# Hybrid decoder layer: the split parts of the attention heads stacked along the rows of the matmul

## The chip, the cores and the metric

The kernel runs on one core of a Trainium2 chip. The metric is the time of one execution on the device, in microseconds (us). Five engines work side by side and meet through semaphores: PE (TensorE, matmuls, with PEld its weight loads), DVE (VectorE), ACT (ScalarE), POOL (GpSimd), and SP, which issues the DMAs. Each engine takes its instructions in order.

## The reference, cut to what matters

One decoder layer, 512 tokens of width 1,024, float32. A combined projection of the normed input, `h @ w_in`, feeds three causal token mixers, an RWKV-7 branch, forgetting attention (the code says fox) and latent attention (mla). Their outputs are gated and merged; an MLP follows. The change lies in the two attentions.

```
# forgetting attention: 4 heads of 64
log_f = jax.nn.log_sigmoid((f + b_forget).astype(jnp.float32))
cum = jnp.cumsum(log_f, axis=1)
s = einsum(q, k) * 64 ** -0.5
s = s + cum[t] - cum[s]            # the decay, per head
# latent attention: 4 heads, 128 columns without position and 64 with rope
s = einsum(concat(q_nope, q_pe), concat(k_nope, k_pe)) * 192 ** -0.5
# both, per block of 128 queries
s = jnp.where(k_pos <= q_pos, s, MASK_VALUE)
p = jax.nn.softmax(s, axis=-1);  o = p @ v
```

## The kernel before

**Split numbers.** A product in float32 is made from float32r parts: `hilo` writes the high part of a tile (ACT) and the rest (DVE), and `mm3` multiplies high by high, high by low and low by high (lines 148 to 150), three passes into one PSUM bank. One *block* is one `mm3` of 128 rows by 512 columns.

**Start.** `startup` norms the input and makes seven 128-row slices of the projection in PSUM (`zps`): five latent slices, and query and key of the first pair of forgetting heads. `attn_inputs` then makes the token-major part (`pn`: values of the forgetting heads, forget logits, rope key), the norms of the latents, query and key of the second pair (`zz`, eight blocks each), and the cumulative log forget (`forget_cumsum`), whose high and low parts for all four heads lie in the rows of `cq` and `ck`.

**Attention loop.** `attention` runs 34 steps: eight heads (0 to 3 forgetting, 4 to 7 latent) times four query blocks j. Step k computes the logits of block k (L_k, keys 0 to 128(j+1)) and its softmax on DVE and ACT, runs filler work, then the product with the values of the head that ended two steps ago (`attend`, every fourth step), then the transposes of the block before (T_(k-1)). The order of PE's instructions is the order in the code; the other engines are ordered by the framework's scheduler from data dependencies.

**Forgetting logits.** The two heads of a pair share a tile, one in rows 0 to 63 and one in rows 64 to 127, so the three passes of a head run on 64 rows. A fourth pass of 128 rows adds the decay (`cq` by `ckh`, where `ckh` picks the head's rows of `ck`), a fifth (identity by mask) the causal mask. The value product takes 128 columns of values, both heads of a pair, in three passes and keeps the 64 rows of its own head.

**Latent logits.** Three passes of 128 rows, then q1 by k1 (high query over both halves, key high and low stacked: 128 rows), then q2 by k1 on 64 rows (low query by high key), then the mask.

**Filler work.** `self.fillers` is a list of (first step, generator). `fill(us)` adds credit and takes pieces from the head of the list while credit lasts and the head's first step has come; credit that finds nothing is dropped. A block is worth `MM3` = 0.64. The amounts are `FILL_0` = 3.9 (before L0, and again in step 0), then per step `FILL_A` = 1.85 plus `FILL_J[k % 4]` = 0.2, -0.2, 0.05, -0.3, and 0.2 more from step 16. `finish(g)` runs the list until g is used up. The pieces are `z_steps(i)`, a 128-row slice of the projection for RWKV (eight blocks); `mla_prep` (rope, queries); `key_norms`; `mla_up(i)`, query and key of latent head i (transposes and five blocks); `mla_values`; and gate slices. Weights come from `self.feed` in the same order, one piece ahead (`weight`): a DMA of 512 KB, then the split into `whi` and `wlo` on ACT and DVE.

```
def finish(self, steps):
    while any(s is steps for _, s in self.fillers):
        next(self.fillers[0][1], None) or self.drop()
```

The buffers that matter: `qk` (queries and keys) has 12, `wk` (softmax rows and scratch) 5, the logits (`sc`) 2, `tp` and `pv` one each, `acc` 3.

## Time and profile before

| | |
|---|---|
| median of 3 runs | 887.59 us (887.14 to 890.51) |
| the profiled execution | 887.63 us, its span 885.9 us |
| PE, PEld | 869.3 us (98%), 706.5 us (80%) |
| DVE, ACT, POOL | 518.8 us (59%), 375.2 us (42%), 98.5 us (11%) |
| granted TensorE clock | 0.993 |
| chain that ended last | PE 89%, DVE 6%, ACT 1%, DMA 1%, issue 1% |
| attention loop | about 99.5 to 242 us of the span |

The span runs from the first to the last instruction. Busy time adds up the intervals of an engine's instructions; matmuls are pipelined, so PE's rows overlap each other. A timeline row gives the start, the duration, the engine, the line, the operation, the tile written, the tiles read, the shape (rows\*columns of the weights and rows x columns of the moving data), and in brackets the idle time before it and what ended it.

### The profile page before, as it was taken

The page shows a single profiled execution, that of the slowest core. Times are in us where ns is not written, and L with a number is a line of the kernel's source. Part 1 is how long each engine was busy: PE and PEld are TensorE (multiplying, and loading weights), DVE is VectorE, ACT ScalarE, POOL GpSimd, SP SyncE. Part 2 cuts the span into 40 slices and gives each one's busy share as a digit, 9 for nine tenths or more (in the row PEclk, how much of TensorE's full clock was granted, in tenths as well). Part 3 has the DMA queues.
Part 4 walks back from the last instruction along what each step waited for, and adds up shares of the span by engine and source line. Part 5 has one row for each costly group of instructions (what it writes and reads, how often), then busy time and mean ns, then how long its engine had stood idle before and what let it go on. Part 6 is the DMA issues. An engine that isn't in the chain of part 4 may idle for free.

```text
span 885.9 us, 12143 instructions
## 1 busy us (share of the span) xinstructions
PE 869.3 (98%) x4568; PEld 706.5 (80%) x4568; DVE 518.8 (59%) x1038; ACT 375.2 (42%) x843; POOL 98.5 (11%) x131
## 2 busy tenths in 40 slices
PE   8889999999999999999999999999999999999997
PEld 6679787877877888886788899888888888888886
DVE  6998775676489765344586696442236543233455
ACT  5357554655462232324654775331314332112331
POOL 4510040000021199100000110000000000000000
PEclk9999999999999999999999999999999999999999
DMA  9764220111246833311147312333346432333311
GB/s 358 231 229 150 74 63 32 53 50 46 91 142 181 280 110 90 113 49 48 32 116 260 118 63 65 116 94 85 104 145 199 132 119 83 96 107 96 95 48 72
DMA packets 32636, 102.57 MB, mean 116 GB/s; under 512 B 5873, under 2 KB 7553, under 8 KB 31810
## 3 DMA queue, kind: packets, MB, share of 16 engines
q1 hardware_dynamic: 32002, 100.94, 36.0%
q0 software_dynamic: 288, 0.79, 0.4%
q8 instruction: 36, 0.59, 0.3%
q14 instruction: 22, 0.18, 0.1%
q10 hardware_dynamic: 288, 0.08, 0.0%
HBM read 99.15 MB, written 2.63 MB: 115 GB/s over the span
## 4 chain that ended last, share of the span: by engine, by line
PE 89%; DVE 6%; ACT 1%; DMA 1%; issue 1%; SPq 0%; DVEq 0%; ACTq 0%
PE acc L148 24%; PE acc L150 24%; PE acc L149 24%; DVE wm L220 1%; PE z L473 1%; PE tp L684 1%; DVE wlo L464 1%; PE sc L148 1%; DVE mod L429 1%; DMA xt<-xT 1%; DVE hl L465 1%; PE sc L717 1%; PE sc L806 1%; PE sc L149 1%; DMA wm<-wmod 1%
## 5 line engine op out<-in xcount | busy, mean ns | idle before, releaser
L121 DVE TENSOR_TENSOR wlo<-wraw,whi 128x512 fp32r<-128x512 f32 (+4 forms) x260 | 167.0, 661 | 209.2 <-ACT whi L120 208.8
L120 ACT ACTIVATE whi<-wraw 128x512 fp32r<-128x512 f32 (+4 forms) x260 | 145.2, 586 | 306.2 <-PE acc L149 180.3
L148 PE MATMUL acc<-g,whi 128*128 128x512 f32 (+1 forms) x304 | 109.4, 360 | 0.0
L150 PE MATMUL acc<-g,wlo 128*128 128x512 f32 (+1 forms) x304 | 109.2, 359 | 0.0
L149 PE MATMUL acc<-g,whi 128*128 128x512 f32 (+1 forms) x304 | 109.2, 359 | 0.0
L148 PE MATMUL acc<-hh,whi 128*128 128x512 f32 x256 | 104.6, 408 | 0.0
L149 PE MATMUL acc<-wlo,uh 128*128 128x512 f32 (+1 forms) x262 | 102.1, 390 | 0.0
L150 PE MATMUL acc<-whi,ul 128*128 128x512 f32 (+1 forms) x262 | 102.0, 389 | 0.0
L148 PE MATMUL acc<-whi,uh 128*128 128x512 f32 (+1 forms) x262 | 102.0, 389 | 0.0
L150 PE MATMUL acc<-hh,wlo 128*128 128x512 f32 x256 | 100.3, 392 | 0.3 <-DVE wlo L121 0.3
L149 PE MATMUL acc<-hl,whi 128*128 128x512 f32 x256 | 100.0, 391 | 0.0
L148 PEld LDWEIGHTS acc<-g,whi 128*128 128x128 f32 x304 | 57.3, 188 | 9.4
L150 PEld LDWEIGHTS acc<-g,wlo 128*128 128x128 f32 x304 | 57.3, 188 | 9.3
L149 PEld LDWEIGHTS acc<-g,whi 128*128 128x128 f32 x304 | 57.3, 188 | 9.2
L220 DVE SCALAR_TENSOR_TENSOR wm<-wm,crow 128x1024 f32<-128x1024 f32 x41 | 50.2, 1225 | 23.2 <-DMA wm<-wmod 23.2
L149 PEld LDWEIGHTS acc<-wlo,uh 128*128 128x128 f32 x262 | 49.3, 188 | 11.6 <-DVE wlo L121 0.4
L148 PEld LDWEIGHTS acc<-whi,uh 128*128 128x128 f32 x262 | 49.3, 188 | 11.1
L150 PEld LDWEIGHTS acc<-whi,ul 128*128 128x128 f32 x262 | 49.3, 188 | 11.1
L150 PEld LDWEIGHTS acc<-hh,wlo 128*128 128x128 f32 x256 | 48.1, 188 | 11.4 <-DVE wlo L121 0.8
L148 PEld LDWEIGHTS acc<-hh,whi 128*128 128x128 f32 x256 | 48.5, 189 | 10.3 <-issue 0.2
L149 PEld LDWEIGHTS acc<-hl,whi 128*128 128x128 f32 x256 | 48.3, 189 | 8.4
L673 ACT ACTIVATE p<-sc,nb 128x128 f32<-128x128 f32 (+3 forms) x32 | 16.8, 525 | 30.0 <-DVE nb L669 16.5
(443 smaller groups left out, 1497.7 us busy)
## 6 DMA issues: line engine op xcount, KB each, us to landing
wm<-wmod SPq DMA_DIRECT2D x36, 512.0 KB, 4.6
wraw<-wu SPq DMA_DIRECT2D x32, 512.0 KB, 3.7
wraw<-wd SPq DMA_DIRECT2D x24, 512.0 KB, 3.5
wraw<-wgb SPq DMA_DIRECT2D x16, 512.0 KB, 3.7
wm<-wmod SPq DMA_DIRECT2D x6, 1024.0 KB, 6.6
wraw<-wz SPq DMA_DIRECT2D x10, 512.0 KB, 3.6
wraw<-wga SPq DMA_DIRECT2D x8, 512.0 KB, 3.6
wraw<-wo SPq DMA_DIRECT2D x8, 512.0 KB, 4.4
```

The costliest lines, as they stand in the source:

```text
L120: nc.scalar.activation(hi, src, AF.Copy)
L121: nc.vector.tensor_tensor(lo, src, hi.bitcast(F32), ALU.subtract)
L148: mm(out, lhs[0], rhs[0], start=start, stop=False)
L149: mm(out, lhs[0], rhs[1], start=False, stop=False)
L150: mm(out, lhs[1], rhs[0], start=False, stop=stop)
L220: self.nc.vector.scalar_tensor_tensor(w, w, 0.5, self.crow[:, cols], ALU.mult, ALU.mult, accum_out=dst)
L429: nc.vector.scalar_tensor_tensor(A, acc[0], b1[:, d:d + 1], self.col("gpre", d), ALU.add, ALU.mult)
L464: nc.vector.tensor_tensor(wlo, raw, whi.bitcast(F32), ALU.subtract)
L465: nc.vector.scalar_tensor_tensor(lo, t, B, hi.bitcast(F32), ALU.add, ALU.subtract)
L473: nc.tensor.matmul(zps[i], w[:, i * P:(i + 1) * P], r, start=first and w is whi and r is hi, stop=last and r is lo)
L673: nc.scalar.activation(p[:, 0:n], ps[:, 0:n], AF.Exp, bias=nb, scale=scale, accum_out=den)
L684: nc.tensor.transpose(tp[:, kb, :], p[:, kb * P:(kb + 1) * P], self.ident)
```

## The change

Queries and keys of each forgetting head get four tiles of 128 rows of their own (`fqa`, `fqb`, `fka`, `fkb`). In `fqa` the head's own 64 rows hold the high part of the query and the other 64 the low part; `fka` holds the high part of the key in both halves. In `fqb` and `fkb` the own rows hold the query's high and the key's low part, and the other rows the decay (`fox_decay`, from `cum` by two constant columns). Two passes of 128 rows then give what four gave. The values of a head are stored as 64 high and 64 low columns side by side; two passes, by the high and by the low part of the probabilities, give a high half and a low half of the output, which `attend` adds. The latent `q2` is stored in both halves, so its pass has 128 rows. Query and key of the second pair move from `attn_inputs` into the filler list (`fox_steps`, from step 4, finished before head 2), and z slices 0 and 1 take their place. `key_norms` is put between the blocks of z[4]. In the constants, `sel` is replaced by `cmul` and `cadd`. The fill amounts stay.

```diff
     def attn_inputs(self, pz, zps):
...
+        self.omu = self.cp.tile([P, 8], F32, name="omu")
+        nc.vector.tensor_scalar(self.omu, self.col("mu", 0, 8), -1.0, 1.0, ALU.mult, ALU.add)
...
-        self.fv = [[self.vt(f"fv{q}{i}") for i in range(2)] for q in "hl"]
+        self.fv = [self.vt(f"fv{t}") for t in range(NT)]
...
-        self.fq = [None, None]
-        self.fk = [None, None]
-        self.fq[0] = (self.qk("fq0h"), self.qk("fq0l"))
-        self.fk[0] = (self.qk("fk0h"), self.qk("fk0l"))
-        self.hilo(*self.fq[0], zps[5], 0.125)
-        self.hilo(*self.fk[0], zps[6])
+        self.fqk = [None] * 4
+        self.fox_queries(0, zps[5])
+        self.fox_keys(0, zps[6])
...
-            vl = slice((t % 2) * 256, (t % 2) * 256 + 256)
-            self.hilo(self.fv[0][t // 2][:, vl], self.fv[1][t // 2][:, vl], pn[t][:, 0:256])
+            fv = self.fv[t].rearrange("p (h q f) -> p h q f", h=4, q=2)
+            self.hilo(fv[:, :, 0], fv[:, :, 1], pn[t][:, 0:256].rearrange("p (h f) -> p h f", h=4))
...
-        gen = self.stream(a["wz"][:, 0:2 * D], D)
-        for i, (dst, name, sc) in enumerate(((self.fq, "fq1", 0.125), (self.fk, "fk1", None))):
+        self.ksq = []
+        self.feed = self.pieces([(a["wz"][:, (2 + i) * D:(3 + i) * D], D) for i in range(2)] + self.attn_weights())
+        self.ahead = None
+        self.weight()
+        for i in range(2):
...
-            for kb, _ in enumerate(self.block_steps(ps, next(gen), h, range(NB))):
+            for kb, _ in enumerate(self.z_steps(i, ps)):
...
-            if i == 0:
-                self.feed = self.pieces(self.attn_weights())
-                self.ahead = None
-            dst[1] = (self.qk(name + "h"), self.qk(name + "l"))
-            self.hilo(*dst[1], ps, sc)
-        self.weight()
...
+    def fox_queries(self, pair, ps):
+        nc = self.nc
+        for hh in range(2):
+            own, oth = slice(hh * 64, hh * 64 + 64), slice(64 - hh * 64, 128 - hh * 64)
+            qa, qb, ka, kb = self.fqk[2 * pair + hh] = [self.qk(n) for n in ("fqa", "fqb", "fka", "fkb")]
+            nc.scalar.activation(qa[own], ps[own], AF.Copy, scale=0.125)
+            nc.vector.scalar_tensor_tensor(qa[oth], ps[own], 0.125, qa[own].bitcast(F32), ALU.mult, ALU.subtract)
+            nc.scalar.activation(qb[own], ps[own], AF.Copy, scale=0.125)
+    def fox_keys(self, pair, ps):
+        nc = self.nc
+        for hh in range(2):
+            own, oth = slice(hh * 64, hh * 64 + 64), slice(64 - hh * 64, 128 - hh * 64)
+            qa, qb, ka, kb = self.fqk[2 * pair + hh]
+            nc.scalar.activation(ka[own], ps[own], AF.Copy)
+            nc.vector.tensor_tensor(kb[own], ps[own], ka[own].bitcast(F32), ALU.subtract)
+            nc.scalar.activation(ka[oth], ps[own], AF.Copy)
+    def fox_decay(self, hd):
+        oth = slice(64 - (hd % 2) * 64, 128 - (hd % 2) * 64)
+        for dst, k in ((self.fqk[hd][1], 4), (self.fqk[hd][3], hd)):
+            self.nc.vector.tensor_scalar(dst[oth], self.cum[oth].bitcast(F32), self.col("cmul", k)[oth],
+                                         self.col("cadd", k)[oth], ALU.mult, ALU.add)
+    def fox_steps(self):
+        for split in (self.fox_queries, self.fox_keys):
+            ps = self.acct()
+            yield from self.block_steps(ps, self.weight(), self.h, range(NB))
+            split(1, ps)
+            yield MM3
+        for hd in (2, 3):
+            self.fox_decay(hd)
     def lat_norm(self, pz, lat, at, n, g):
...
-        nc.vector.tensor_copy(self.lfx[:, :, :, 0:4], self.lf[:, :, None, :].broadcast_to([P, NT, 4, 4]))
+        for at in (0, 4):
+            nc.vector.tensor_copy(self.lfx[:, :, :, at:at + 4], self.lf[:, :, None, :].broadcast_to([P, NT, 4, 4]))
...
-        self.cq = self.qk("cq")
-        self.ck = wk("ck")
-        nc.gpsimd.memset(self.ck, 1.0)
-        nc.gpsimd.tensor_copy(self.cq, self.ck)
     def forget_cumsum(self, pz):
-        nc, cq, ck = self.nc, self.cq, self.ck
+        nc = self.nc
...
-        chi = self.wk("chi").bitcast(F32R)
-        nc.scalar.activation(chi, pc, AF.Copy)
-        nc.vector.tensor_copy(cq[0:32], pc[0:32])
-        nc.vector.tensor_tensor(cq[32:64], pc[32:64], chi[32:64].bitcast(F32), ALU.subtract)
-        nc.vector.tensor_scalar(ck[64:96], chi[64:96].bitcast(F32), -1.0, None, ALU.mult)
-        nc.vector.tensor_tensor(ck[96:128], chi[96:128].bitcast(F32), pc[96:128], ALU.subtract)
+        self.cum = cum = self.wk("cum").bitcast(F32R)
+        nc.scalar.activation(cum, pc, AF.Copy)
+        for rows in (slice(32, 64), slice(96, 128)):
+            nc.vector.tensor_tensor(cum[rows], pc[rows], cum[rows].bitcast(F32), ALU.subtract)
+        for hd in range(2):
+            self.fox_decay(hd)
     def attn_weights(self):
...
-        return [z(0), z(1), z(2), (a["wqr"], 768), z(3), z(4), up(0), z(5), up(1), (a["wv"], D), up(2), z(6), up(3),
+        return [z(2), z(-2), z(-1), (a["wqr"], 768), z(3), z(4), up(0), z(5), up(1), (a["wv"], D), up(2), z(6), up(3),
...
     def attention(self):
...
-        self.omu = self.cp.tile([P, 8], F32, name="omu")
-        nc.vector.tensor_scalar(self.omu, self.col("mu", 0, 8), -1.0, 1.0, ALU.mult, ALU.add)
-        z = [self.z_steps(i) for i in range(8)]
+        z = [self.z_steps(i) if i > 1 else None for i in range(8)]
+        fox = self.fox_steps()
...
-        self.fillers = [(0, z[0]), (0, z[1]), (0, z[2]), (0, prep), (0, z[3]), (0, z[4]), (0, self.key_norms()), (12, up[0]), (0, z[5]),
+        self.fillers = [(0, z[2]), (4, fox), (0, prep), (0, z[3]), (0, self.between(z[4], self.key_norms())), (12, up[0]), (0, z[5]),
...
-        self.gbc, self.ga, self.ksq = [], [], []
+        self.gbc, self.ga = [], []
...
+                    if hd == 2:
+                        self.finish(fox)
...
+    def between(self, main, side):
+        for cost in main:
+            next(side, None)
+            yield cost
+        for _ in side:
+            pass
     def softmax(self, st, j):
...
-            self.mm3(pv[:, kb * P:], st["vof"](kb), (pt[0][:, sl], pt[1][:, sl]), kb == 0, kb == NT - 1)
+            v = st["vof"](kb)
+            if len(v) == 2:
+                self.mm3(pv[:, kb * P:], v, (pt[0][:, sl], pt[1][:, sl]), kb == 0, kb == NT - 1)
+            else:
+                for i in range(2):
+                    self.nc.tensor.matmul(pv[:, kb * P:], v[0], pt[i][:, sl], start=kb == 0 and i == 0,
+                                          stop=kb == NT - 1 and i == 1)
...
-        self.nc.scalar.activation(self.y[st["dst"]][rows], pv[rows], AF.Copy)
+        y = self.y[st["dst"]][rows]
+        if len(v) == 2:
+            self.nc.scalar.activation(y, pv[rows], AF.Copy)
+        else:
+            low = self.wk("low")[0:64]
+            self.nc.scalar.activation(low, pv[64:128], AF.Copy)
+            self.nc.vector.tensor_tensor(y, pv[0:64], low, ALU.add)
...
         def start():
-            nc, cq, ck, identr, cmaskr = self.nc, self.cq, self.ck, self.identr, self.cmaskr
+            nc, identr, cmaskr = self.nc, self.identr, self.cmaskr
...
-            q, k = self.fq[hd // 2], self.fk[hd // 2]
-            ckh = self.qk("ckh")
-            nc.vector.tensor_scalar(ckh, ck, self.col("sel", hd), None, ALU.mult)
+            qa, qb, ka, kb = self.fqk[hd]
             def logits(j, ps):
...
-                self.mm3(ps, (q[0][rows, ql], q[1][rows, ql]), (k[0][rows, 0:n], k[1][rows, 0:n]), True, False)
-                nc.tensor.matmul(ps, cq[:, ql], ckh[:, 0:n], start=False, stop=False)
+                nc.tensor.matmul(ps, qa[:, ql], ka[:, 0:n], start=True, stop=False)
+                nc.tensor.matmul(ps, qb[:, ql], kb[:, 0:n], start=False, stop=False)
...
-            half = slice((hd // 2) * P, (hd // 2) * P + P)
-            vof = lambda kb: tuple(f[kb // 2][:, (kb % 2) * 256:][:, half] for f in self.fv)
+            vof = lambda kb: (self.fv[kb][:, hd * P:hd * P + P],)
...
-        nc.vector.tensor_tensor(q2[0:64], pq[0:64], q1[0:64].bitcast(F32), ALU.subtract)
+        for half in (slice(0, 64), slice(64, 128)):
+            nc.vector.tensor_tensor(q2[half], pq[0:64], q1[0:64].bitcast(F32), ALU.subtract)
...
-                nc.tensor.matmul(ps, q2[0:64, ql], k1[0:64, 0:n], start=False, stop=False)
+                nc.tensor.matmul(ps, q2[:, ql], k1[:, 0:n], start=False, stop=False)
...
-            yield 0.4
+                yield 0.1
...
-    def z_steps(self, i):
+    def z_steps(self, i, ps=None):
...
-        ps = self.acct()
+        ps = self.acct() if ps is None else ps
```

More of the change, by code (lines that the diff above doesn't have):

```diff
@@ L81 @@
     ("mu", 8), ("a0", 2), ("k_k", 2), ("k_a", 2), ("r_k", 2), ("ln_g", 2), ("ln_b", 2),
-    ("qg", 3), ("kvg", 2), ("bf", 4), ("sel", 4), ("invf", 32),
+    ("qg", 3), ("kvg", 2), ("bf", 4), ("cmul", 5), ("cadd", 5), ("invf", 32),
 ))
@@ L1516, in _constants @@
     msk = np.concatenate([strict, incl, incl], axis=1).astype(np.int32)
-    sel = np.zeros((P, 4), np.float32)
+    cmul, cadd = np.zeros((P, 5), np.float32), np.zeros((P, 5), np.float32)
+    row = i % 32
+    cmul[row < 4, 4], cadd[(row >= 4) & (row < 8), 4] = 1.0, 1.0
     for h in range(4):
-        sel[h::32, h] = 1.0
-    return cst, msk, sel
+        cmul[row == 4 + h, h], cadd[row == h, h] = -1.0, 1.0
+    return cst, msk, cmul, cadd
 def layout(x, c, positions, w_in, mu_shift, w0, w_decay_up, a0, w_aaa_up, w_gate_up, k_k, k_a, r_k, ln_x_g, ln_x_b,
@@ L1527, in layout @@
     c_ = np.ascontiguousarray
-    cst, msk, sel = _constants()
+    cst, msk, cmul, cadd = _constants()
     ins = {"cst": cst, "msk": msk}
@@ L1541, in layout @@
         "r_k": tcol(r_k), "ln_g": tcol(ln_x_g), "ln_b": tcol(ln_x_b), "qg": tcol(q_norm_g), "kvg": tcol(kv_norm_g),
-        "bf": np.tile(arr(b_forget).reshape(1, 4), (P, 1)), "sel": sel,
+        "bf": np.tile(arr(b_forget).reshape(1, 4), (P, 1)), "cmul": cmul, "cadd": cadd,
         "invf": np.tile(np.float32(10000.0) ** (-np.arange(0, 64, 2, dtype=np.float32) / np.float32(64)), (P, 1)),
```

## The prediction

> **What bounds the kernel now.** I read the page first, then the stretch of the attention loop, then the TensorE rows around the logits.
>
> ```profile
> span 885.9 us, 12143 instructions
> PE 869.3 (98%) x4568; PEld 706.5 (80%) x4568; DVE 518.8 (59%) x1038; ACT 375.2 (42%) x843; POOL 98.5 (11%) x131
> ```
>
> TensorE is busy for 98% of the span. The table by stretches says the same of the loop that the change rewrites (columns: length, then busy time of PE, PEld, DVE, ACT, POOL, then the granted clock and DMA):
>
> ```profile
> 104.00:236.00 132.00, 131.50 (x684) 104.99 (x684) 83.56 (x210) 69.17 (x164) 10.44 (x26) 1.00 0.18 54
> ```
>
> PE has work in 131.5 of 132.0 us, at full clock; DVE and ACT have about 40% room. So a microsecond taken from PE is a microsecond of the result, and a wait put on PE is one lost. Busy time overlaps in this view (matmuls are pipelined), so I cost PE by the step from one start to the next. One group of forgetting logits, last query block (512 keys), with its neighbours, and the ends of a first-block group (128 keys), in order of time:
>
> ```profile
> 117.08 0.38 PE L684 MATMUL tp<-ident,p 128*128 128x128 f32 x2
> 117.39 0.49 PE L148 MATMUL sc<-fk0h,fq0h 64*128 64x512 f32 x1
> 117.73 0.39 PE L149 MATMUL sc<-fk0l,fq0h 64*128 64x512 f32 x1
> 117.96 0.39 PE L150 MATMUL sc<-fk0h,fq0l 64*128 64x512 f32 x1
> 118.28 0.50 PE L717 MATMUL sc<-ckh,cq 128*128 128x512 f32 x1
> 118.62 0.22 PE L718 MATMUL sc<-cmaskr,identr 128*128 128x128 f32 x1
> 118.68 0.45 PE L148 MATMUL acc<-hh,whi 128*128 128x512 f32 x1
> ...
> 121.23 0.33 PE L148 MATMUL sc<-fk0h,fq0h 64*128 64x128 f32 x1
> 121.99 0.33 PE L148 MATMUL acc<-whi,lath 128*128 128x256 f32 x1
> ```
>
> A 512-column pass costs 0.23 where the passes around it have the same rows (117.73 to 117.96), but 0.32 and 0.34 where the rows change between 64 and 128. The latent-attention group has one 64-row pass (L806):
>
> ```profile
> 180.17 0.38 PE L684 MATMUL tp<-ident,p 128*128 128x128 f32 x2
> 180.30 0.48 PE L148 MATMUL sc<-knh,qnh 128*128 128x512 f32 x1
> 180.62 0.40 PE L149 MATMUL sc<-knl,qnh 128*128 128x512 f32 x1
> ...
> 181.08 0.40 PE L805 MATMUL sc<-k,q 128*128 128x512 f32 x1
> 181.41 0.49 PE L806 MATMUL sc<-k,q 64*128 64x512 f32 x1
> 181.83 0.33 PE L807 MATMUL sc<-cmaskr,identr 128*128 128x128 f32 x1
> 181.99 0.45 PE L148 MATMUL acc<-whi,lath 128*128 128x512 f32 x1
> ...
> 185.44 0.27 PE L805 MATMUL sc<-k,q 128*128 128x128 f32 x1
> 186.06 0.45 PE L148 MATMUL acc<-whi,lath 128*128 128x512 f32 x1
> ```
>
> **What it takes away.** *Forgetting logits.* A head's four groups (16 groups in all) step 0.76, 0.83, 1.06 and 1.29, first and last quoted: 3.9 us. The lead-in after two transposes is 0.31 against 0.13 for the 128-row group, so 0.18 more for each: 4.6 us a head. Afterwards a group has two passes of 128 rows and the mask: 0.32 + 0.23 + 0.06 = 0.61 for 512 keys, and by the same rows at 128, 256 and 384 keys 0.36, 0.38 and 0.49, so 1.84 a head. Saved 2.8 x 4 heads = 11.1. Ends: 5.0 if only two plain passes go (0.23, 0.17, 0.12, 0.11 each, 1.26 a head), 11.5 at best. I take 11.1, since all its rows stand here.
>
> *Values.* Four key blocks of 512, 384, 256 and 128 columns make 1,280 a head; one of three passes over them goes, at 0.23 per 512 columns (rows above): 0.57 a head, 2.3 for four. The added sum of the two halves (one DVE operation a head) lies beside the next step's fill; without that cover its price would be one DVE row of 0.68 (quoted below).
>
> *Latent logits.* From L805 to the next work 0.91 at 512 keys and 0.62 at 128. With all passes alike: 0.23 + 0.23 + 0.06 = 0.52 and 0.33. Saved over the four sizes 0.29, 0.38, 0.39, 0.39 = 1.45 a head, 5.8 in all; the ends are 0 and 5.8. The extra half of q2 is one more DVE operation a head.
>
> *Key norms* put between z[4]'s blocks: the same 16 matmuls, 1.9 busy. I take nothing; the ends are 0.9 either way.
>
> ```profile
> L819 PE MATMUL acc<-cstt,ksq 128*128 128x2 f32 x16 | 1.9, 249 | 0.0
> ```
>
> Together 19.2 us off PE.
>
> **What it moves, and the waits.** Fill credit is arithmetic that can be walked by hand: each block of three passes is worth 0.64 and takes 3 x 0.23 = 0.69 us; each step buys about 1.85. Before, z[0], z[1], z[2] (24 blocks) feed the first fills up to step 3. Now z[0] and z[1] run ahead of the loop in the place of the second query/key pair, and the queue starts with z[2] (8 blocks) and then `fox`, which may not begin before step 4. Seven blocks go before L0, one in step 0; then steps 0 to 3 find nothing, and their credit is dropped. All later work shifts: `fox` has 4 of its 16 blocks left when head 2 begins (step 8, forced there by `finish`), up[0] runs whole in `finish` at step 16, up[1]'s last block at 20, the last two blocks of up[2] end only a transposition ahead of step 24, and up[3]'s last runs at 28. At the end of the loop both versions have done 11 gate blocks, so nothing is carried past it. The moved weight loads keep their order of use, one block ahead, with cover of 5.5 us (8 blocks) against a landing of
>
> ```profile
> wraw<-wz SPq DMA_DIRECT2D x10, 512.0 KB, 3.6
> ```
>
> and cost nothing; without that cover it would be up to 3.6 each. PE is in order, so behind each wait stands everything.
>
> *Up-projections (waits at 16, 20, 24, 28).* The trace has the nearest case, step 28 before: last block of up[3], then one block of z[7] and three transposes, then the logits.
>
> ```profile
> 216.75 0.39 PE L150 MATMUL acc<-lath,wlo 128*128 128x512 f32 x1
> ...
> 217.67 0.49 PE L684 MATMUL tp<-ident,p 128*128 128x128 f32 x3
> 218.02 0.33 PE L148 MATMUL sc<-knh,qnh 128*128 128x128 f32 x1
> 218.85 0.33 PE L149 MATMUL sc<-knl,qnh 128*128 128x128 f32 x1 [0.50 <-DVE knl L121]
> ```
> ```profile
> 217.38 0.59 ACT L120 ACTIVATE knh<-acc 128x512 fp32r<-128x512 f32 x1
> ```
> ```profile
> 218.12 0.68 DVE L121 TENSOR_TENSOR knl<-acc,knh 128x512 fp32r<-128x512 f32 x1
> ```
>
> The last pass of the projection to the second logits pass took 2.1, about 0.2 of it ACT finishing other work; PE lost 0.7 (0.83 from 218.02 to 218.85, of which the pass itself is about 0.1) with 1.04 of cover (0.69 and the 0.35 from 217.67). With none it loses about 1.6: 1.6 x 3, and 1.25 at step 24 (0.35 of transposes) is 6.05, less the 0.7 already paid, 5.4; ends 4.3 (each 0.3 less) and 7.5 (DVE behind at step 16, where two q2 halves, qnl, the scaling and the splits of the next weight queue up). I take 5.5.
>
> *Head 2 (step 8).* After the last key block ACT must write both halves of `fka` (first pass), DVE then the low part and two decay rows (second pass). An ACT write of 64 rows costs as much as one of 128:
>
> ```profile
> L784 ACT ACTIVATE q<-pq x4: 589/592/594, 156.0 to 213.0; 64x512 fp32r<-64x512 f32 x4
> ```
>
> First pass 0.4 + 2 x 0.5 after the block; less its own step, a wait of 1.4 (low end); with DVE's 0.68 and the decay rows behind it up to 3.5. I take 2.3, two DVE operations past the low end.
>
> *Steps 1 to 3, no fill.* PE stands until each softmax is through. From 118.62 (mask) to the end of the scaling here
>
> ```profile
> 120.95 0.49 DVE L675 TENSOR_SCALAR p<-p,rden 128x512 f32<-128x512 f32 x1
> ```
>
> is 2.8, 0.3 of it behind a ckh. Smaller blocks have less to reduce and to raise:
>
> ```profile
> L669 DVE TENSOR_REDUCE nb<-sc x32: 275/484/692, 105.3 to 233.0; 128x1 f32<-128x128 f32 x8, 128x1 f32<-128x256 f32 x8, 128x1 f32<-128x384 f32 x8, 128x1 f32<-128x512 f32 x8
> L673 ACT ACTIVATE p<-sc,nb x32: 351/521/690, 105.6 to 233.9; 128x128 f32<-128x128 f32 x8, 128x256 f32<-128x256 f32 x8, 128x384 f32<-128x384 f32 x8, 128x512 f32<-128x512 f32 x8
> ```
>
> so about 1.7, 1.9 and 2.3 for blocks 0 to 2. The PE work between logits and transposes covers 1.1, 1.2 and 1.55, leaving 0.6 + 0.7 + 0.75 = 2.05 (low end). z[2]'s evictions and the split of the next weight share the same ACT and DVE: 3.0, high end 4.5.
>
> *Start of the attention inputs.* Four ACT writes in the place of one for each of query and key, 6 more at about 0.5 (3 us), and 2 more on DVE, ahead of `nh` for the third weight block. It is late already:
>
> ```profile
> PEld n L149 <- DVE nl L121: 0.6, 2, 0.4
> ```
>
> Two square operations of about 0.5 may fall behind it and a little slack is there: 1.3, ends 0 and 2.5. *The rest:* attend(4) takes values straight after the last value block, 0.3 (0 to 0.6); extra ACT and DVE work in steps 4 to 8, 0.3 (0 to 1).
>
> *The clock.* A pause of PE is followed by a stretch at half clock:
>
> ```profile
> 46.57 2.48 PE L473 MATMUL z<-hh,whi 128*128 128x512 f32 x7 [2.14 <-ACT hh L463]
> ```
> ```profile
> 48.00:51.00 3.00, 3.00 (x9) 2.32 (x8) 2.93 (x5) 1.41 (x4) 1.21 (x1) 0.50 0.66 265
> ```
>
> A 2.14 us pause, then 0.50 for about 3 us: some 1.6 of work lost. The waits above come near that in steps 1 to 3 and 8; I take one such stretch, 1.6; ends 0 and five stretches, 8. [...]
>
> **Sum.** Added: 5.5 + 2.3 + 3.0 + 1.3 + 0.3 + 0.3 + 1.6 = 14.3. Taken away: 19.2. Net -4.9 against the profiled execution's own 887.63 (span 885.9), which stands level with the median of 887.59: 882.7.
>
> **The rivals.** *The waits are only the bare dependencies* (7.7 at their low ends, clock kept): 887.63 - 19.2 + 7.7 = 876.1. For it: DVE and ACT have 40% room in the loop. Against it: at step 28 ACT was busy just when it mattered. *The clock drops at most of the waits*: without the one stretch the net is -6.5, each costs 1.6, and from the fifth on the kernel is slower than before; five give 889.1. There are seven places. For it the 2.14 us pause; against it, the 0.5 wait of step 28 had no such effect (clock 1.00 in the loop). *The steps around the 64-row passes do not go with the rows* (they would belong to the change of operand, say): then only the plain passes go, 5.0 + 2.3 = 7.3, and the result is 887.63 - 7.3 + 14.3 = 894.6; it decides as soon as less than 14.3 of the 19.2 is real. Against it: the same change of operand at 180.17 to 180.30 and 180.62 costs no more than 0.13. [...]
>
> **Chances.** A measurement here tells about 0.5% from no change: 883.2 and 892.0 are the bounds. Forecast 0.50 (own range 878 to 887, 0.28 of it below 883.2, 0.22 within); bare dependencies 0.22 (faster); clock 0.18 (0.14 within, 0.04 slower, with further stretches or the high ends); steps stay 0.07 (slower); something else within 0.03. So faster 0.50, same 0.39, slower 0.11. The range goes from the bare case, 875.5, to just past the clock case, 890.
>
> **What would show it.** Logits groups of 0.36 to 0.61 us with three matmuls, latent groups without the 0.33 and 0.42 steps, two passes in pv; PE idle on softmax rows just after the first logits, on `fka`, `fkb` or decay rows at head 2, on `knl` or `knh` at heads 4 to 7, on `nl` at the third weight block; dips of granted clock behind them. I am wrong if the groups keep steps of 0.3 between equal rows, if the waits add up to less than 10 or more than 18, or if waits appear past the attention loop.

## The result and the profile after

The changed kernel takes 898.32 us (median of 4 runs, 897.79 to 900.54) against 888.23 for the kernel before in the same measurement (887.14 to 890.51): ratio 1.0115, 95% interval 1.0088 to 1.0142. The forecast was 882.7 in a range of 875.5 to 890. The profiled execution took 897.9, its span 896.1, its clock 0.980.

The line of busy times from the page after, and the row for the attention loop (columns as before: length, then busy time of PE, PEld, DVE, ACT, POOL, then granted clock and DMA):

```profile
PE 863.1 (96%) x4520; PEld 705.8 (79%) x4520; DVE 527.8 (59%) x1053; ACT 382.5 (43%) x855; POOL 94.7 (11%) x129
```
```profile
104.00:236.00 132.00, 116.75 (x587) 97.23 (x586) 86.84 (x208) 67.48 (x158) 9.38 (x26) 0.91 0.16 50
```

In the same 132 us PE ran 587 matmuls where it ran 684 before (the change itself takes only 48 out of the whole kernel), was without work for 15 us, and had 0.91 of its clock. What was meant to become faster did. A forgetting group of 512 keys and a latent one, in TensorE's timeline after:

```profile
123.96 0.38 PE L718 MATMUL tp<-ident,p 128*128 128x128 f32 x2
124.09 0.48 PE L760 MATMUL sc<-fka,fqa 128*128 128x512 f32 x1
124.41 0.39 PE L761 MATMUL sc<-fkb,fqb 128*128 128x512 f32 x1
124.64 0.22 PE L762 MATMUL sc<-cmaskr,identr 128*128 128x128 f32 x1
124.70 0.45 PE L148 MATMUL acc<-hh,whi 128*128 128x512 f32 x1
...
181.33 0.40 PE L850 MATMUL sc<-k,q 128*128 128x512 f32 x1
181.56 0.22 PE L851 MATMUL sc<-cmaskr,identr 128*128 128x128 f32 x1
```

The forgetting group takes 0.61 us, the q2 pass 0.23, and the lead-in after two transposes 0.13: the values of the prediction to the hundredth. The loss is in the waits of the loop (waits of PE after, 104 to 236 us: total, times, longest):

```profile
PE sc L148 <- ACT knh L120: 5.3, 4, 2.2
PE tp L718 <- DVE p L709: 3.1, 2, 2.6
PE sc L760 <- ACT fka L557: 2.4, 1, 2.4
PE sc L149 <- DVE knl L121: 2.3, 4, 0.6
PE tp L718 <- DVE nb L705: 1.7, 2, 0.9
PE tp L718 <- DVE ptl L723: 0.4, 2, 0.3
```

and in what follows them. The stretches of the loop at half clock, from the table by stretches, with the bounds set where the clock changes:

```profile
110.11:116.94 6.83, 6.25 (x19) 5.13 (x20) 3.89 (x12) 2.68 (x8) 0.00 (x0) 0.50 0.26 79
134.00:137.41 3.41, 3.41 (x19) 3.41 (x17) 1.89 (x7) 1.05 (x3) 2.97 (x14) 0.50 0.43 139
168.14:171.55 3.41, 3.41 (x11) 2.83 (x11) 1.29 (x5) 0.46 (x2) 0.00 (x0) 0.50 0.53 159
188.62:192.03 3.41, 3.41 (x9) 2.63 (x9) 1.12 (x5) 1.05 (x3) 0.00 (x0) 0.50 0.52 154
209.10:212.51 3.41, 3.41 (x10) 2.61 (x9) 0.45 (x2) 0.30 (x2) 0.00 (x0) 0.50 0.48 154
229.58:232.99 3.41, 3.41 (x10) 2.63 (x9) 0.46 (x3) 0.46 (x2) 0.00 (x0) 0.50 0.49 154
```

PE is busy nearly all of each of these, at half speed (a 512-column pass steps 0.43 from 114.05 to 114.48, and 0.23 from 117.22 to 117.45, at full clock): six stretches, behind steps 2, 8, 16, 20, 24 and 28, the first 6.83 us long and the others 3.41. PE works in 23.3 us of them, so they cost at most half of that, 11.7. A busy share alone hides this; the clock column shows it.

To see the parts apart, I took the TensorE timeline from the first logits (L0) to the first pass of L31 and added the steps (start to the next start) by the tile written, with the waits taken out. The kernels from the experiments below stand beside it.

| us | L0 to L31 | logits `sc` | filler `acc` | `tp` | `pv` | waits |
|---|---|---|---|---|---|---|
| before | 126.7 | 35.1 | 68.1 | 8.2 | 12.9 | 0.5 |
| after | 136.4 | 23.5 | 78.2 | 7.1 | 10.5 | 15.2 |
| pauses filled | 126.8 | 21.9 | 81.6 | 6.1 | 10.5 | 4.9 |
| order only | 146.6 | 37.3 | 75.4 | 8.7 | 13.0 | 10.4 |
| second order, evened | 117.4 | 21.4 | 72.1 | 6.6 | 11.0 | 4.5 |

The filler is the same work before and after, as the rows of its tile say:

```profile
104.37:231.06 126.69, 73.21 (x314) 53.14 (x313) 16.67 (x28) 12.25 (x20) 1.00 0.18 52
```
```profile
105.33:241.68 136.35, 82.56 (x314) 60.03 (x313) 17.80 (x30) 15.57 (x26) 0.91 0.16 48
```

The same 314 matmuls took 10.1 us longer, nearly all of it by the clock: 19.4 us of them lie in the six stretches, and half of that is 9.7. Set beside the kernel whose pauses are filled, logits and transposes took 1.6 and 1.0 longer: 12.7 in all, of which the stretches explain at most 11.7; the cause of the other 1.0 stays open. At full clock the change saved 13.2 on the logits, 2.1 on the lead-ins and 2.4 on the values, 17.7. So 14.7 more waits, plus the 12.7, less 17.7, is 9.7: the 9.66 by which L0 to L31 grew. These are differences within one table, so their sum closes by itself; the second order below shows the saving again. L0 itself is 0.96 later, and from L31 to the end nothing changed (654.8 before, 654.4 after).

### The profile page after: what moved, and what is told of

Read it like the earlier page. It is cut to its first block, busy times and chain, and to the rows that moved or that the text cites. A ratio compares the mean times of both kernels' runs of the same rounds, so it can differ in the third digit from the quotient of the medians.

```text
span 896.1 us, 12076 instructions
## 1 busy us (share of the span) xinstructions
PE 863.1 (96%) x4520; PEld 705.8 (79%) x4520; DVE 527.8 (59%) x1053; ACT 382.5 (43%) x855; POOL 94.7 (11%) x129
## 4 chain that ended last, share of the span: by engine, by line
PE 84%; DVE 10%; ACT 2%; issue 2%; DMA 1%; SPq 0%; DVEq 0%; ACTq 0%
PE acc L148 24%; PE acc L149 23%; PE acc L150 23%; PE z L473 2%; DVE wlo L121 1%; PE tp L718 1%; DVE wm L220 1%; DMA xt<-xT 1%; DVE wlo L464 1%; PE pr L1187 1%; PE pu L1028 1%; DVE mod L429 1%; DVE hl L465 1%; DVE q L829 0%; PE py L1204 0%
## 5 line engine op out<-in xcount | busy, mean ns | idle before, releaser
L148 PE MATMUL acc<-hh,whi 128*128 128x512 f32 x256 | 108.0, 422 | 0.0
L149 PE MATMUL acc<-hl,whi 128*128 128x512 f32 x256 | 102.4, 400 | 0.0
L150 PE MATMUL acc<-hh,wlo 128*128 128x512 f32 x256 | 102.3, 400 | 0.0
L220 DVE SCALAR_TENSOR_TENSOR wm<-wm,crow 128x1024 f32<-128x1024 f32 x41 | 50.1, 1223 | 23.3 <-DMA wm<-wmod 23.3
L148 PEld LDWEIGHTS acc<-hh,whi 128*128 128x128 f32 x256 | 50.0, 195 | 10.4 <-issue 0.2
```

Source lines behind the costliest of these rows:

```text
L148: mm(out, lhs[0], rhs[0], start=start, stop=False)
L149: mm(out, lhs[0], rhs[1], start=False, stop=False)
L150: mm(out, lhs[1], rhs[0], start=False, stop=stop)
L220: self.nc.vector.scalar_tensor_tensor(w, w, 0.5, self.crow[:, cols], ALU.mult, ALU.mult, accum_out=dst)
```

## The experiments

The theory (A): the moved blocks make products end too close to their readers; PE waits, and the half clock behind the waits costs about as much again. Against it: that the stacking itself or the load on ACT and DVE is the cause. Each ratio is to the kernel before in the same measurement (medians 887.84, 889.46 and 889.61 in the three).

**Order only.** The kernel before with the moves of the change and without any stacking.

```diff
-        for i, (dst, name, sc) in enumerate(((self.fq, "fq1", 0.125), (self.fk, "fk1", None))):
+        for i in range(2):
...
+            for kb, _ in enumerate(self.z_steps(i, ps)):
...
-        self.fillers = [(0, z[0]), (0, z[1]), (0, z[2]), (0, prep), (0, z[3]), (0, z[4]), (0, self.key_norms()), (12, up[0]), (0, z[5]),
+        self.fillers = [(0, z[2]), (4, fox), (0, prep), (0, z[3]), (0, self.between(z[4], self.key_norms())), (12, up[0]), (0, z[5]),
...
+                    if hd == 2:
+                        self.finish(fox)
```

> The kernel before with only the order of the change: z slices 0 and 1 ahead of the loop, query and key of the second pair as filler work from step 4, key norms between the blocks of z[4]; passes and splits as before. Theory A: the waits come with the order, 10 to 14 us, and 4 to 6 half-clock stretches of 1.7 us behind them: 903 to 912 us. Theory B: as before, 887 to 890 us.

909.61 (907.52 to 910.97, 4 runs), ratio 1.0241 (1.0219 to 1.0262). The waits of its loop (104 to 250 us) and the loop's row:

```profile
PE sc L148 <- ACT knh L120: 4.6, 4, 2.2
PE sc L149 <- DVE knl L121: 2.2, 4, 0.7
PE tp L699 <- DVE p L690: 2.0, 1, 2.0
PE sc L148 <- ACT fk1h L120: 1.0, 1, 1.0
PE sc L149 <- DVE fk1l L121: 0.5, 1, 0.5
```
```profile
104.00:236.00 132.00, 121.65 (x595) 95.38 (x594) 74.89 (x185) 62.60 (x148) 9.42 (x26) 0.95 0.16 45
```

The order alone costs 21.8 us, and the changed kernel, which has the stacking too, 10.1: so in this order the stacking is worth about 11.7, not the 17.7 taken off PE. The waits that theory A expected (10 to 14) came at 10.4, and its half-clock stretches too, four of them, 17.1 us long. The rest of the saving shows in the change's larger sums: its waits are 15.2 against these 10.4, and its stretches 23.9 us long against 17.1. Here, work taken off PE in front of the waits made them longer.

**Pauses filled.** The changed kernel with 49 spare products of 512 columns, results unused, in its pauses (the expectation says 44, but its own list adds up to 49).

```diff
+HOLD_L = {8: 10, 16: 10, 20: 4, 24: 5, 28: 5}
+HOLD_T = {1: 2, 2: 11, 3: 2}
...
+    def hold(self, n):
+        ps = self.acct()
+        for _ in range(n):
+            self.nc.tensor.matmul(ps, self.h[0][0][:, 0:P], self.h[0][1], start=True, stop=True)
```

> The changed kernel with 44 spare matmuls of 512 columns put where PE waits (2, 11 and 2 before the transposes of steps 1 to 3; 10, 10, 4, 5, 5 before the first logits of heads 2, 4, 5, 6, 7); their result is used by nothing, and they add about as much PE work as there was idle time. Theory A1 (the half clock follows from the idle time and is lost time of its own): the granted clock stays at 1.00 from 104 to 240 us and about 11 us go, 886 to 890 us, though every wait is still there. Theory A2 (the waits alone cost the time, the clock is a mere record): 898 us or up to 2 more.

889.6 (888.81 to 890.17, 10 runs), ratio 1.0014 (1.0002 to 1.0027).

```profile
104.00:236.00 132.00, 126.86 (x685) 105.92 (x684) 92.38 (x223) 71.74 (x168) 9.51 (x26) 1.00 0.17 50
```

Nothing useful was added and the kernel is 1.0% faster than the change, about 9 us: the clock is 1.00 throughout. By the table, waits are 10.3 less, spare work is 13.5 more and the 12.7 are regained: 9.5 from L0 to L31. Waits and spare work together keep PE from its work for 18.4 us, where the waits alone took 15.2, so the gain does not come from shorter pauses: the half clock is a cost of its own. The time lies in theory A1's range.

**One stretch.** The same, with the 15 spare products of steps 1 to 3 only (`HOLD_T`).

> After, with spare 512-column products (15, results unused) only in the pauses of steps 1 to 3. It measures the half-clock stretch behind them by itself. Theory A (a stretch of about 3.3 us at half clock costs 1.6 us, as the prediction priced it): clock 1.00 in the window from 104 to 122 us where it was 0.81, and 1 to 2 us less than after: 896.3 to 897.3. Theory B (the clock's loss there is cover that a later wait takes back): the clock comes back to 1.00 and the time stays within 0.5 us of after.

895.02 (893.81 to 896.83, 5 runs), ratio 1.0064 (1.0047 to 1.0082), against 1.0115 for the change: the intervals just miss each other.

```profile
104.00:122.00 18.00, 17.98 (x94) 14.58 (x93) 12.68 (x33) 8.73 (x24) 0.00 (x0) 1.00 0.20 59
```

L0 to L31 is 133.80, 2.55 less than after. Theory A was right on the clock and low on the gain (1 to 2): its 1.6 was for about 3 us at half clock, and this stretch lasts 6.83, with PE busy for 6.25, so it can cost up to 3.1. The ratios are 4.5 us apart, more than the trace shows.

**First new order.** The changed kernel with z[4] and the preparation put ahead of the forgetting blocks, so that steps 1 to 3 have fill and the up-projections come earlier.

```diff
...
-        self.fillers = [(0, z[2]), (4, fox), (0, prep), (0, z[3]), (0, self.between(z[4], self.key_norms())), (12, up[0]), (0, z[5]),
+        self.fillers = [(0, z[2]), (0, z[4]), (0, prep), (4, fox), (0, z[3]), (0, self.between(z[5], self.key_norms())), (12, up[0]),
                         (16, up[1]),
```

> The changed kernel with the filler list re-ordered so that no early step goes without work and no up-projection is late: z[2], z[4], the rope preparation, then fox from step 4, z[3], z[5] with the key norms, up[0] and so on. The stacked passes are as in the change. Theory A (the order starves PE: waits, and half clock behind them, eat a saving that is there): the waits of steps 1 to 3 (about 4 us), most of those before heads 4 to 7 (about 8) and five of six half-clock stretches (about 10) go, the wait before head 2 stays: 873 to 879 us. Theory B (the extra splits on ACT and DVE and the stacked operands themselves cost the time): no better than 890.

888.64 (886.88 to 891.75, 10 runs), ratio 1.0004 (0.9990 to 1.0017): 1.1% better than the change, but far off theory A's 873 to 879 and barely better than theory B's 890. Its waits (104 to 236 us):

```profile
PE tp L718 <- DVE ptl L723: 4.3, 3, 1.9
PE sc L760 <- ACT fka L557: 2.4, 1, 2.4
PE acc L148 <- DVE rope L779: 1.6, 1, 1.6
PE sc L148 <- ACT knh L120: 1.4, 1, 1.4
...
PE sc L149 <- DVE knl L121: 0.5, 1, 0.5
```

The up-projection waits fell from 7.6 to 1.9, but DVE now has the rope of the preparation in the short first steps, and PE waits for it and for the transposes' low parts behind it. Three half-clock stretches of 3.41 us were left (from 124.14, 144.62 and 175.34 us). Whether these waits come from the five `wk` buffers as well as from DVE's load was not tried apart.

**ScalarE's copies first.** The wait of 2.4 at head 2 looked longer than its parts. ACT's rows ahead of it:

```profile
130.82 0.57 ACT L555 ACTIVATE fka<-acc 64x512 fp32r<-64x512 f32 x1
131.29 0.62 ACT L120 ACTIVATE whi<-wraw 128x512 fp32r<-128x512 f32 x1
132.26 0.59 ACT L557 ACTIVATE fka<-acc 64x512 fp32r<-64x512 f32 x1 [0.35 <-DVE fkb L556]
```

ACT stands 0.35 for DVE (and 0.76 at the other head), though both read `acc`. The subtraction also reads the `fka` that the copy goes on writing; but in `fox_queries`, where the second copy writes a tile of its own, ACT stands just so (0.38 at 125.88, 0.78 at 127.85). The two reads were thus taken in turn here, as the code has them; the row shows ACT released by DVE's operation. What two reads at once would cost, no run here shows. So I put the second copy ahead of the subtraction, in `fox_keys` and likewise in `fox_queries`.

```diff
             nc.scalar.activation(ka[own], ps[own], AF.Copy)
+            nc.scalar.activation(ka[oth], ps[own], AF.Copy)
             nc.vector.tensor_tensor(kb[own], ps[own], ka[own].bitcast(F32), ALU.subtract)
-            nc.scalar.activation(ka[oth], ps[own], AF.Copy)
```

> After, with the second ScalarE copy of each key and query half issued ahead of the VectorE subtraction that reads the same product. Theory A (the two engines read one product in turn, in the order of the code, and that lengthens the wait at head 2): the wait of 2.4 us at the head's first logits falls to 1.2 to 1.6 us, maybe a half-clock stretch goes with it, 895 to 897.5. Theory B (the chain of the two engines is as long in either order): the wait stays at 2.2 to 2.6 us and the time at 897.5 to 899.

899.23 (898.4 to 900.55, 5 runs), ratio 1.0114 (1.0091 to 1.0138): no change.

```profile
134.26 0.33 PE L760 MATMUL sc<-fka,fqa 128*128 128x128 f32 x1 [1.57 <-ACT fka L556]
134.98 0.33 PE L761 MATMUL sc<-fkb,fqb 128*128 128x128 f32 x1 [0.39 <-DVE fkb L557]
```

The wait for `fka` fell as expected, to 1.57; 0.39 came back at the next pass and 0.96 at a transposition of step 7, and the half clock behind it stayed. Theory A was right on the order of the reads and wrong on the time.

**The parts by themselves.** The kernel before with only the values stacked (the `fv` tiles, `attend` and its sum):

> Before, with only the values of the four forgetting heads stacked (two passes for three, no change of order). Theory A (the saved passes are worth what the prediction worked out, where the order is left alone): 2.3 us less, 885.0 to 886.0, and the four value groups of heads 0 to 3 each about 0.6 us shorter. Theory B (the extra copy and addition behind each value product hold up the next one, or the loop gives the time back elsewhere): 887 to 889.

885.61 (884.02 to 887.28, 12 runs), ratio 0.9959 (0.9945 to 0.9973). A value product of heads 0 to 3 takes 1.22 instead of 1.85; L0 to L31 is 124.30 for 126.69, 2.4 less. The ratio's 2.4 to 4.9 takes that in.

The kernel before with only `q2` in both halves:

```diff
-        nc.vector.tensor_tensor(q2[0:64], pq[0:64], q1[0:64].bitcast(F32), ALU.subtract)
+        for half in (slice(0, 64), slice(64, 128)):
+            nc.vector.tensor_tensor(q2[half], pq[0:64], q1[0:64].bitcast(F32), ALU.subtract)
...
-                nc.tensor.matmul(ps, q2[0:64, ql], k1[0:64, 0:n], start=False, stop=False)
+                nc.tensor.matmul(ps, q2[:, ql], k1[:, 0:n], start=False, stop=False)
```

> The kernel before with only q2 stored in both halves, so that the latent logits have no 64-row pass. By the step rows 5.8 us go: 882.4 us beside 888.2. If the long steps do not go with the rows: 888, no change.

884.24 (882.17 to 886.76, 10 runs), ratio 0.9956 (0.9941 to 0.9971). The logits fell by 5.1 up to L31, of 5.4 worked out; L0 to L31 fell by 3.0. The rest shows in two places: head 7 now waits 1.18 where it waited 0.50 (first and second pass of step 28), and a stretch ran at half clock that no pause had preceded:

```profile
216.31 0.33 PE L148 MATMUL sc<-knh,qnh 128*128 128x128 f32 x1 [0.68 <-ACT knh L120]
217.14 0.33 PE L149 MATMUL sc<-knl,qnh 128*128 128x128 f32 x1 [0.50 <-DVE knl L121]
```
```profile
152.90 1.89 PE L820 MATMUL acc<-cstt,ksq 128*128 128x2 f32 x16
```
```profile
154.93:158.34 3.41, 3.41 (x13) 2.52 (x11) 2.08 (x6) 2.24 (x6) 0.00 (x0) 0.50 0.35 99
```

The sixteen key norms, two columns each, lie just ahead. That they are the cause was not shown by itself, but the traces speak for it. In these traces the clock changes only at edges 3.41 us apart (last section). Here the whole bunch lies between two of them, 151.52 and 154.93. In the kernel before and in the one with the values alone, an edge cuts the same bunch (into 0.77 and 1.12 us, and 1.05 and 0.85), and no half clock follows.

**Both parts that need no new order**, with the key norms spread over z[4] and up[3] ahead of z[6]:

```diff
...
-        self.fillers = [(0, z[0]), (0, z[1]), (0, z[2]), (0, prep), (0, z[3]), (0, z[4]), (0, self.key_norms()), (12, up[0]), (0, z[5]),
-                        (16, up[1]), (18, values), (20, up[2]), (0, z[6]), (24, up[3]), (0, z[7]),
+        self.fillers = [(0, z[0]), (0, z[1]), (0, z[2]), (0, prep), (0, z[3]), (0, self.between(z[4], self.key_norms())), (12, up[0]),
+                        (0, z[5]), (16, up[1]), (18, values), (20, up[2]), (23, up[3]), (0, z[6]), (0, z[7]),
...
```

> Before, with the two parts of the change that need no new order of blocks: the values stacked, and q2 in both halves; the key norms spread over block 4 as in the change, and up-projection 3 ahead of block 6. Theory A (these parts give what their passes take, once the wait at head 7 and the half clock behind the bunched key norms are gone): 2.3 + 5.8 us less than before, ratio 0.9905 to 0.9925, and no half clock in the loop. Theory B (each part alone gave 3.6 to 3.9 us, and together they run into the same limit): ratio 0.9935 to 0.996.

880.69 (880.36 to 881.29, 4 runs), ratio 0.9904 (0.9884 to 0.9924): 8.5 us by the ratio, against 8.1 that their passes take, so theory A. No wait at head 7 and no half clock; one wait is new, 0.96 at a value product:

```profile
104.00:236.00 132.00, 130.92 (x707) 108.37 (x706) 89.54 (x221) 71.84 (x169) 10.44 (x26) 1.00 0.21 61
```

**Second new order.** The changed kernel with z[2] to z[4] first, and every product ended at least a step ahead of its reader.

```diff
...
+        self.fillers = [(0, z[2]), (0, z[3]), (0, self.between(z[4], self.key_norms())), (4, fox), (0, prep), (0, z[5]), (12, up[0]),
+                        (0, z[6]), (16, up[1]), (18, values), (20, up[2]), (23, up[3]), (0, z[7]),
...
+                if k == 7:
+                    self.finish(fox)
                 if j == 0:
-                    if hd == 2:
-                        self.finish(fox)
```

> After, with another order of the blocks in the loop: blocks 2, 3 and 4 first, with key norms in the third; then the forgetting blocks of heads 2 and 3, closed one step before head 2; then the preparation, block 5, up-projection 0, block 6, up-projection 1, the values, up-projections 2 and 3, block 7. Every product has then at least one step between its end and its first reader. Theory A (the waits and the half clock that follows them are all that ate the saving): no wait of over 0.6 us in the loop, clock 1.00 throughout, 869 to 877. Theory B (with shorter logits each step is too short for its softmax chain on VectorE and ScalarE, whatever the order): transposes wait 1 to 2 us in several steps as in the first new order, clock under 0.97 in part of the loop, 882 to 890.

885.66 (879.59 to 886.67, 12 runs), ratio 0.9942 (0.9921 to 0.9962): 1.7% better than the change, and faster than before. The time is theory B's, the trace is more like theory A's: the clock is 1.00 throughout the loop and no transposes wait, though 3.3 us of waits remain, 1.57 the longest. L0 to L31 takes 117.90, 18.5 less than after. (The profiled execution took 881.48, one of the quicker of the twelve.) But a new pause stands behind the loop, at the first RWKV product, with 3.41 us of half clock from 237.86:

```profile
237.98 3.59 PE L961 MATMUL pdl<-rww,tw 128*128 128x256 f32 x8 [3.59 <-POOL U L1016]
```

The same order with ScalarE's copies first:

> The same new order with the second ScalarE copy of each half also ahead of the VectorE subtraction. Theory A: the head 2 wait is already covered there, so the same time as the new order alone, within 0.5 us. Theory B (the serial chain also delays the softmax of the steps beside it): 1 to 3 us less than the new order alone.

884.66 (880.62 to 887.08, 10 runs), ratio 0.9951 (0.9932 to 0.9970): no difference that these intervals can show, as theory A had it (its half a microsecond is finer than they are). The pause behind the loop is there too, 3.47, and 10.24 us of half clock behind it.

The second order with nothing stacked:

> Before, with only the second new order of the blocks (2, 3, 4, the forgetting blocks, the preparation, 5, up-projection 0, 6, and so on), nothing stacked. Theory A (the order of the change was dear because its products ended too close to their readers; an order that keeps a step between them costs nothing): no wait of over 1 us in the loop beside the one at the preparation, 885 to 891, so that stacking in this order is worth 3 to 8 us. Theory B (any order that moves blocks out of the loop's start costs something): 893 to 900.

894.87 (893.02 to 900.13, 6 runs), ratio 1.0077 (1.0049 to 1.0104). By time theory B, by the trace neither: the loop waits 0.7 us at clock 1.00, but the pause behind it is there too, and half clock behind the pause (the profiled execution took 899.98, 5.1 above the median; four of the six took 893.0 to 895.6 at a higher mean clock):

```profile
252.53 3.75 PE L932 MATMUL pdl<-rww,tw 128*128 128x256 f32 x8 [3.70 <-DMA rww<-rww]
```
```profile
236.00:300.00 64.00, 59.00 (x289) 45.80 (x290) 48.04 (x99) 25.33 (x51) 8.78 (x8) 0.89 0.44 133
```

This order runs 341 filler matmuls between L0 and L31 where the kernel before runs 314: nine gate blocks are drawn into the loop, and less work is left to cover the transfer of `rww` behind it. (The trace names the transfer here and with ScalarE's copies first; in the second order with stacking it names a POOL write. Only the cover was tried, in the next run.) Stacking in this order is worth 1.35%, 12 us. Between L0 and L31, at full clock in both, it takes 133.2 to 117.9, with 18.0 less in logits, lead-ins and values: the 17.7 from above, in another order.

**Second order, evened.** The same with all stacking, and `FILL_MLA` 0.0 in place of 0.2, so that gate blocks remain for that pause.

> After in the second new order, with the extra filler credit of 0.2 us for each of the 16 latent steps set to nothing, so that about five steps of gate blocks are left for the time after the loop. Theory A (the 3.6 us pause at the first RWKV product and others behind it come from gate blocks used up too early): the pause goes, the loop ends about 3 us earlier, 1 to 4 us less than the second order alone, ratio to before 0.990 to 0.993. Theory B (that pause waits for a transfer whatever lies ahead, and the latent steps now end in waits): the same or 1 to 3 us more than the second order alone.

878.0 (875.95 to 879.15, 4 runs), ratio 0.9870 (0.9850 to 0.9890): the fastest of all here, 11.6 us below the kernel before. The pause went from 3.59 to 0.85, and 326 filler matmuls lie between L0 and L31. Theory A was right on the pause and low on the gain, 0.7% between the two ratios, 6 us. The half clock behind the pause went with it, 3.41 us in the one trace of the second order; what it cost in the other executions no trace shows.

```profile
104.00:236.00 132.00, 126.65 (x692) 108.20 (x692) 95.73 (x232) 77.50 (x180) 9.50 (x26) 0.99 0.22 63
...
236.00:300.00 64.00, 62.89 (x349) 50.35 (x350) 56.60 (x120) 24.16 (x49) 10.42 (x12) 1.00 0.64 196
```

Of the 11.6 us, 8.5 came already with the two parts that need no new order. The forgetting logits stacked without moving any blocks were not run; four tiles for each of four heads are sixteen, and `qk` has twelve.

## Why the prediction was wrong

*What it takes away:* right. 18.8 of the 19.2 lay before L31, and 17.7 came, the values at 2.4 for 2.3, logits with lead-ins at 15.3 for 16.5. That the steps around 64-row passes go with the rows is settled by the groups and by the run with `q2` alone (5.1 of 5.4).

*What the moves cost, without the clock:* nearly right in total, partly by luck.

| term | predicted | measured | from |
|---|---|---|---|
| up-projections, steps 16 to 28 | 5.5 | 7.1 | 5.3 + 2.3, less the 0.5 of before |
| transposes ahead of steps 20 and 28 | none | 1.7 | wait for `nb` |
| head 2 | 2.3 | 2.4 | wait for `fka` |
| steps 1 to 3 | 3.0 | 3.1 | wait for `p` |
| start of the attention inputs | 1.3 | 1.0 | L0 at 105.33 for 104.37 |
| the rest | 0.6 | 0.4 | wait for `ptl` |
| the clock | 1.6 | 12.7 | the step sums; the stretches explain at most 11.7 |

The order of the blocks and the places of these waits came as walked. Two totals fit by luck. In steps 1 to 3, I had 0.6 to 0.75 each and about 1 for shared engines; 0.52, 2.60 and nothing came, since in step 2 DVE did an eviction (0.74) and two weight splits (1.28) ahead of the scaling. At head 2 I had 1.4 at the first pass and DVE's share at the second; all 2.43 came at the first, with a weight split (0.62) and the 0.35 of standing for DVE between ACT's two copies (rows above). And the 1.0 is one execution's: with the same code up to L0, two others have it at 105.76 and 106.46. The up-projections missed by 1.6, inside their range. The longest of their waits, 2.2 at step 16, has more behind it than the DVE work that I named; ACT's rows:

```profile
161.37 1.28 ACT L869 ACT_TABLE_LOAD   x1
...
162.79 1.14 ACT L120 ACTIVATE whi<-wraw 128x512 fp32r<-128x512 f32 x2
...
166.24 0.59 ACT L120 ACTIVATE knh<-acc 128x512 fp32r<-128x512 f32 x1
```

The key norms' square root loads a table just ahead of that step, 1.28 us, and ACT has no pause from there to `knh`; what the wait would be without it was not tried. The 1.7 at the transposes ahead of steps 20 and 28 was not in my sum at all.

*The clock:* this is the step that failed, by its count. I had the mechanism (a pause, then half clock), a row for it, seven places (eight by my own list of waits), and a rival with five stretches; I took one stretch. Six came, the first of them twice as long: seven lengths of 3.41 us, where I had paid for one. The price was about right, at most 1.7 for a length where I had 1.6; together that is at most 11.7, and the step sums say 12.7. I gave no ground for one. What I held against more, that the 0.5 wait of step 28 did not lower the clock before, spoke of a pause a third to a fifth as long as those I forecast; the 2.14 us row was the nearer one for waits of 1.6 to 2.5, and by it four or five places were to be expected. Nor is it the single pause that counts: at heads 5 to 7 the longest were 0.86, 1.20 and 1.02, each with another of 0.51 to 0.60 close behind, and the half clock came all the same (last section).

With the measured terms the sum is 28.4 added and 18.1 taken away (17.7 and the 0.4 of L31 itself): 10.3 more, and the span grew by 10.2. All of them are read from the same two traces, so this is an account and not a test. The rival of many stretches (889.1, 0.18) was the right one, with its five lengths too few. The bound that the waits add up to 10 to 18 held; the sign of the whole did not.

## What to carry to other kernels

Where one engine is busy all the time, a change of order is not paid for by the saved work alone: the pauses it opens cost their length, and here the half clock behind them cost nearly as much again (14.7 us of added waits, at most 11.7 by the six stretches). Work saved in front of a wait came back here as a longer wait (15.2 us of waits with the stacking, 10.4 with the order only), so first keep a step of other work between a product and its reader, and leave filler for the next transfer behind the loop; so ordered, the whole change took 1.3% off the kernel instead of adding 1.2%. Price the half clock by the idle time that falls close together, not by the longest pause (in these traces 1.20 and 0.51 us in one window of 3.41 brought it, and a single 1.81 that an edge cut did not), and count every place rather than take one for all.

## What the hardware showed

In each of the fourteen traces of this case the clock changes only at edges 3.41 us apart. Until the last one at the program's end, every stretch of half clock is 3.41 us long or two, three or four times that (6.83, 10.24, 13.65), and within one execution their starts lie whole multiples of 3.41 apart. After, these are 110.11, 134.00, 168.14, 188.62, 209.10 and 229.58.

What counts, in these traces, is how long PE is without work between two edges, in one pause or in several. Between 60 and 300 us, 948 such windows began at full clock. The 23 with 1.6 us or more of idle PE were all followed by half clock. Of the 919 with less than 1.4, one was, the window with the bunched key norms. Of the six between, four were. So at head 6 the 1.20 and the 0.51 counted together (PE busy 1.81 of 3.41 from 205.69), while single pauses of 1.61, 1.81 (first new order, ending at 118.34 and 169.14) and 1.79 (second order, ScalarE's copies first) were each cut by an edge and brought no half clock. In the first 60 us a window with only 0.36 idle (10.09 to 13.51 in the kernel before) was followed by half clock as well, so 1.6 is a reading of this loop and not a fixed limit.

A pause of 1.57 us, at the same place in two kernels with the same code up to there, was followed by half clock in one (evened, the first three rows) and not in the other (second order). Each pause lies whole within one window; each kernel's wait, then that window and the next:

```profile
141.80 0.39 PE L148 MATMUL acc<-whi,lath 128*128 128x256 f32 x1 [1.57 <-ACT fka L557]
```
```profile
139.16:142.57 3.41, 1.84 (x15) 1.53 (x14) 3.33 (x9) 2.14 (x4) 0.09 (x1) 1.00 0.30 80
142.57:145.98 3.41, 3.41 (x19) 3.41 (x17) 2.38 (x9) 0.93 (x3) 2.49 (x6) 0.50 0.04 16
```
```profile
142.28 0.39 PE L148 MATMUL acc<-whi,lath 128*128 128x256 f32 x1 [1.57 <-ACT fka L557]
```
```profile
138.87:142.29 3.42, 1.85 (x16) 1.55 (x14) 3.34 (x8) 2.89 (x6) 0.00 (x0) 1.00 0.06 10
142.29:145.70 3.41, 3.41 (x30) 3.41 (x31) 3.41 (x12) 1.39 (x5) 2.48 (x6) 1.00 0.24 86
```

What decides so near the limit, these traces do not show.

The edges fall at other times from trace to trace: 134.00 after and 142.57 evened are 8.57 us apart, two and a half times 3.41. So the same pauses were cut by an edge in one trace and not in another: the 0.86 and 0.56 at head 5 were followed by half clock after, and not in the run with one stretch filled, where an edge at 185.85 falls among them. The 12 executions of the second order ran from 879.6 us at a mean clock of 0.992 to 886.7 at 0.983.
